# Hybrid layer with product-key experts on one core: a gathered row placed inside the weighing, the attention's normalisation placed earlier, one LayerNorm block split by tiles, and expert weights loaded 11 transfers ahead

## The chip, the cores and the metric

The kernel runs on one core of a Trainium2 chip. The metric is the device time of one execution in microseconds (us); lower is better. Engines are named as in the profile: PE (matrix multiply), PEld (its weight loads), DVE (vector), ACT (scalar), POOL (GpSimd), SP (its queue issues most transfers).

## The reference, cut to what matters

One layer: an input projection feeds a gated recurrence, a convolution and a grouped attention with rotary positions; their merged outputs go through a projection and a LayerNorm (norm 1); then come product-key experts and norm 2. The change touches the attention, norm 1 and above all the experts:

```python
v1, i1 = lax.top_k(s1, PEER_TOPK); v2, i2 = lax.top_k(s2, PEER_TOPK)
...
score, ci = lax.top_k(cand, PEER_TOPK)        # 16 of 16384 experts for each token and head
g = jax.nn.softmax(score, axis=-1)
act = jax.nn.gelu(jnp.einsum('thkd,td->thk', u_tab[expert], t))
return jnp.einsum('thk,thkd->td', g * act, v_tab[expert])
```

There are 512 tokens, 8 heads of 16 experts, and 16384 experts with two rows of 1024 numbers each (tables u and v).

## The kernel before, in words

All matrix products are made of three matmuls on numbers split into a high part (`whi`, `ph`, made by ACT) and a low part (`wlo`, `pl`, made by DVE as number minus high part). The order of work on PE, DVE, ACT and POOL is the order of the code; each of these engines works its list off strictly in order. The order of SP's transfers is made by a scheduler, but SP too works its list off in order.

**Experts.** The experts are done in two ways at once.

- Tokens 0 to 127 gather. For each of the 128 pairs of head and rank one transfer, issued by POOL, fetches 128 rows (512 KB, tile `raw`) of u, later of v. `gather_step` uses one such transfer: for u a product with the tokens (L1489), for v a multiply and add into `ttok` (L1497). I call one of these a row operation. 14 of the 256 are done before the stages below; the rest are spread over the steps below by a budget (`shares`), 1.18 in a step at first and 3.22 later.
- Tokens 128 to 511 are done densely: 128 groups of 128 experts. For group n, `first` multiplies the weights u(n) with the tokens (24 matmuls into `pa`), ACT applies the gelu (tile `a`), `weigh` multiplies it by the gates (`gr`, L1602) and splits the product into `ph` and `pl` (L137, L138), and `second` multiplies it with v(n) (18 matmuls into `acc`). For groups 0 to 70 the gelu output was made earlier and kept: 32 in SBUF (tile `arun`, named `gt` in the profile), 39 in DRAM (`ad`).

The main loop runs over steps i. Step i weighs group i + 1 and runs `second` for group i. I name three stretches of it. **Stage A1** is steps 0 to 31, whose activations lie in SBUF. **Stage A2** is steps 32 to 68, whose activations are read back from DRAM (192 KB each). **Stage B** is steps 69 to 122, each of which also runs one `first`.

Weights come through `wload`: one 512 KB transfer into one of three buffers `wraw` (L124), two halves cast by ACT (L129) and two low parts (L131). `fetch` calls it when a step wants the group. When `arun` has been read, its space takes the 11 tiles of norm 2 (`fin`), eight of which `prepare` fills by transfers of 512 KB, starting at i = 96 in the code; SP's list has them much earlier, where the space comes free. `prepare` then runs eight vector operations on them (L1679, L1682).

**Attention.** A slot n of 32 handles one head and block of queries: the softmax of slot n + 1 is started, the scores of n + 2 multiplied, and `turn` transposes the probabilities `P` of slot n. `norm` divides `P` by its sum (L947, L948). Parts of the next heads' projections, rotations (`rope`) among them, are slipped in as `early` and `late`.

**Norm 1.** `modulate` scales the transposed block by channel: eight 128x128 pieces in two tiles `tf` of four, some on DVE (L1172), some on ACT (L1170). PE's next products (`pu`) need the high part of block 3 (L1179).

Of the kernel before, what the change touches and what calls it, by code (L numbers as in the profile page):

```python
# [9 lines left out]
F32 = mybir.dt.float32  # L10
# [7 lines left out]
AF = mybir.ActivationFunctionType  # L18
# [4 lines left out]
T, TC, D, KT = 512, 256, 1024, 8  # L23
NB, NBC = T // 128, TC // 128
H = 8
# [69 lines left out]
def body(tc, I, O):  # L95
    nc = tc.nc
# [39 lines left out]
    def split(hi, lo, src):  # L136
        A.activation(hi, src, AF.Copy)  # L137
        V.tensor_sub(lo, src, hi.bitcast(F32))  # L138
# [76 lines left out]
    u = hc.tile([128, KT, T], F32, name="u")  # L215
# [105 lines left out]
    def go(*gens):  # L321
        for g in gens:
            next(g, None)
# [239 lines left out]
    def norm():  # L563

        bc = pms.tile([128, T], F32, name="ms")
        P.matmul(bc, ones[:, 0:1].to_broadcast([128, 128]), usum, start=True, stop=True)
        qsum = hp.tile([128, T], F32, name="scT")
        last = None
        for j in range(KT):
            uj = u[:, j, :]  # L570
            V.scalar_tensor_tensor(uj, bc, -1.0 / D, uj, op0=ALU.mult, op1=ALU.add)
            sq = hp.tile([128, T], F32, name="KM")
            A.activation(sq, uj, AF.Square)
            if j:
                G.tensor_add(qsum, last, sq)
            last = qsum if j else sq
            if j % 3 == 2:
                yield
        yield
        st = pms.tile([128, NB], F32, name="ms")  # L580
        for b in range(NB):
            P.matmul(st[:, b:b + 1], qsum[:, b * 128:(b + 1) * 128], ones, start=True, stop=True)
        t1 = const.tile([128, NB], F32, name="lt")
        rs = const.tile([128, NB], F32, name="lrs")
        pspow(rs, st, 1.0 / D, t1)
        yield
        uhl.extend([mp.tile([128, KT, T], F32R, name="uhi"), hc.tile([128, KT, T], F32R, name="og")])
        bc = pst.tile([128, NB, 128], F32, name="bc")
        for b in range(NB):
            P.matmul(bc[:, b, :], rs[:, b:b + 1].to_broadcast([128, 128]), ident, start=True, stop=True)  # L590
        bc = bc[:].rearrange("p b t -> p (b t)")
        V.tensor_mul(u[:, 0, :], u[:, 0, :], bc)
        yield
        for j in range(KT):
            uj = u[:, j, :]
            if j + 1 < KT:
                V.tensor_mul(u[:, j + 1, :], u[:, j + 1, :], bc)
            s = mp.tile([128, T], F32, name="ms", bufs=2)
            A.activation(s, uj, AF.Sigmoid, scale=chan['clg'][:, j:j + 1], bias=chan['clb'][:, j:j + 1])
            V.tensor_scalar(uj, uj, chan['clg'][:, j:j + 1], chan['clb'][:, j:j + 1], op0=ALU.mult, op1=ALU.add)  # L600
            V.tensor_mul(uj, uj, s)
            A.activation(uhl[0][:, j, :], uj, AF.Copy)
            if j:
                V.tensor_sub(uhl[1][:, j - 1, :], u[:, j - 1, :], uhl[0][:, j - 1, :].bitcast(F32))
            yield
        V.tensor_sub(uhl[1][:, KT - 1, :], u[:, KT - 1, :], uhl[0][:, KT - 1, :].bitcast(F32))
        yield
# [358 lines left out]
    def slot(n, early=(), late=(), mid=(), pre=()):  # L966

        h, b = divmod(n, NB)
        norm(h, b)
        if n + 1 < NB * H:  # L970
            softmax(*divmod(n + 1, NB))
        go(*pre)
        if n + 2 < NB * H:
            scores(*divmod(n + 2, NB))
        fetch_next()
        if b == 0 and h:
            out(h - 1)
        go(*early)
        fetch_next()
        go(*mid)  # L980
        turn(b)
        go(*late)
        fetch_next()

# [178 lines left out]
    def modulate(b, pts):  # L1163
        tfs = []
        for q_, pt in enumerate(pts):
            tf = op.tile([128, 4, 128], F32, name="tf", bufs=4)
            for i in range(4):
                j = q_ * 4 + i
                if j > 4 if b == 3 else q_:
                    A.activation(tf[:, i, :], pt[:, i, :], AF.Identity, scale=gs[:, j:j + 1], bias=bs[:, j:j + 1])  # L1170
                else:
                    V.tensor_scalar(tf[:, i, :], pt[:, i, :], gs[:, j:j + 1], bs[:, j:j + 1], op0=ALU.mult, op1=ALU.add)  # L1172
            tfs.append(tf)
        return tfs
# [94 lines left out]

    vrows = I['v'].rearrange("(a b) d -> a b d", b=128)  # L1270

    def fetch(item):
        kind, i = item
        src = {'q': I['wq'], 'u': I['uT'], 'v': None}[kind]
        src = vrows[i] if kind == 'v' else src[i]
        if kind != 'q':
            src = src.rearrange("p (k e) -> p k e", e=128)
        UV[item] = wload(src, SUBS[kind])

    ad = tc.dram_tile([NU - NA, 128, TD], F32, name="ad")  # L1280

# [309 lines left out]

    ph = {}

    def halves(i2, a_):
        names = ("raw", "raw") if i2 >= NT - 2 else ("ph", "pl")
        ph[i2] = [pp.tile([128, TD], F32R, name=n, bufs=RB[1] if n == "raw" else 2) for n in names]
        split(ph[i2][0], ph[i2][1], a_)

    def weigh(n, a_):

        v_ = a_.rearrange("p (b t) -> p b t", t=GB)
        V.tensor_tensor(v_, v_, gates[n // GN][:, :, n % GN, :], op=ALU.mult)  # L1602
        halves(n, a_)
        if n % GN == GN - 1:
            del gates[n // GN]
        read_gates(n)
# [21 lines left out]
    def shares(i):  # L1628

        n = min(2 * NS_, EARLY + int(share * sum(budget[:i + 1])))  # L1630
        out = [gather_step] * (n - gathered[1])
        gathered[1] = n
        return out

    todo = []

# [85 lines left out]
    for i in range(NT - LAST):  # L1722
        n = i + 1
        todo += shares(i)
        left = 6
        if NU <= n:
            fetch(('u', n + 1))
            left = 10
            a_ = first(n, left)
        else:  # L1730
            if n + 1 == NU:
                fetch(('u', NU))
            if NA <= n + 1 < NU:
                back[n + 1] = gap.tile([128, TD], F32, name="a", bufs=4)
                nc.sync.dma_start(back[n + 1], ad[n + 1 - NA])
            weigh(n, arun[:, n, :] if n < NA else back.pop(n)[:])
        if ('v', n) not in UV:
            fetch(('v', n))
        for m in range(2):
            for b in range(NB - 1):  # L1740
                second(i, b, m)
                some(6 - 3 * m - b)
        if NU <= n:
            weigh(n, a_[:])
        if i >= NT - 32:
            prepare(i - NT + 32)
        if gathered[0] == 2 * NS_ and 0 not in nst:
            residual(0, 0)
            residual(0, 1)
            moments(0)  # L1750
            norm2(0, 0)
            norm2(0, 1)
        del UV['v', i], ph[i]
# [42 lines left out]
```

## Time and profile before

| | before |
|---|---|
| median of 3 runs | 2436.23 us (2435.23 to 2440.38) |
| the profiled execution | 2440.56 us, span 2438.8 us |
| mean granted TensorE clock | 0.990 |
| busy over the span | PE 96%, PEld 83%, DVE 79%, ACT 43%, POOL 27% |
| bytes moved by the DMA engines | 452.66 MB |

A busy share is an average over stages with different limits, and PE's is also flattered, since the ends of pipelined matmuls are modelled and overlap. What a stage is worth is read from its own length, and from how far apart the same instruction starts in neighbouring steps.

### The profile page before, as it was taken

The numbers are of one execution on the slowest core, as the hardware profiler recorded it, in microseconds if no ns is written. First come the engines' busy times: TensorE is split into PE (matmuls) and PEld (weight loads), VectorE is DVE, ScalarE is ACT, GpSimd is POOL, SyncE is SP. The second block draws the span as 40 slices with busy tenths as digits, with TensorE's granted clock in tenths as the row PEclk, the third lists the DMA queues.
The fourth block names the chain that finished last, engine by engine and source line by source line (L and its number), as shares of the span: only waits on it lengthen the run. The fifth ranks groups of instructions, "written<-read, shape, count | busy, mean of one in ns | idle before, by whom it ended". The sixth has DMA issues, their size and how long they took to land.

```text
span 2438.8 us, 34766 instructions
## 1 busy us (share of the span) xinstructions
PE 2344.7 (96%) x12547; PEld 2022.8 (83%) x12547; DVE 1935.6 (79%) x3736; ACT 1043.3 (43%) x2294; POOL 648.6 (27%) x555
## 2 busy tenths in 40 slices
PE   7999999999999999999999999999989999999997
PEld 3888888887887777877999999987767888898886
DVE  7788888887875566564999699968878788889886
ACT  5544444443423444643366645533333333332333
POOL 6000000002111000041688301122323344444432
PEclk9999999999999999999999999999999999999999
DMA  6211111111482111242323379999999989998962
GB/s 241 74 61 61 60 54 61 61 61 64 163 303 76 35 35 35 70 145 81 104 98 111 123 259 324 327 331 307 349 354 348 351 320 336 339 333 317 337 220 93
DMA packets 156973, 452.66 MB, mean 186 GB/s; under 512 B 16256, under 2 KB 60672, under 8 KB 154624
## 3 DMA queue, kind: packets, MB, share of 16 engines
q1 hardware_dynamic: 106976, 278.33, 32.9%
q0 software_dynamic: 36864, 134.23, 15.5%
q10 hardware_dynamic: 12960, 37.87, 4.1%
q8 instruction: 99, 1.62, 0.3%
q14 instruction: 74, 0.61, 0.1%
HBM read 411.77 MB, written 37.03 MB: 184 GB/s over the span
## 4 chain that ended last, share of the span: by engine, by line
PE 60%; DVE 24%; DMA 7%; ACT 5%; issue 3%; POOL 2%; ACTq 0%; DVEq 0%; POOLq 0%; SPq 0%
PE mm L142 13%; PE mm L144 13%; PE mm L143 13%; DVE wlo L131 6%; DVE raw L1489 4%; DMA wraw<-in_v_dram 3%; PE sc L455 2%; PE pg L1539 2%; ACT whi L129 2%; PE acc L142 2%; PE acc L143 2%; PE acc L144 2%; ACT ph L137 2%; DMA wraw<-in_uT_dram 2%; DVE ttok L1497 2%
## 5 line engine op out<-in xcount | busy, mean ns | idle before, releaser
L131 DVE TENSOR_TENSOR wlo<-wraw,whi 128x512 fp32r<-128x512 f32 x687 | 465.1, 719 | 156.3 <-ACT whi L129 155.0
L142 PE MATMUL mm<-xh,wlo 128*128 128x512 f32 (+1 forms) x1448 | 555.9, 384 | 12.4 <-POOL wlo L131 3.8
L143 PE MATMUL mm<-xl,whi 128*128 128x512 f32 (+1 forms) x1448 | 536.9, 371 | 2.1 <-DVE xl L1180 0.9
L144 PE MATMUL mm<-xh,whi 128*128 128x512 f32 (+1 forms) x1448 | 537.3, 371 | 0.0
L129 ACT ACTIVATE whi<-wraw 128x512 fp32r<-128x512 f32 x784 | 448.5, 621 | 98.7 <-DMA wraw<-in_v_dram 22.6
L142 PE MATMUL acc<-whi,pl 128*128 128x512 f32 x756 | 300.6, 398 | 24.1 <-DVE pl L138 17.2
L142 PEld LDWEIGHTS mm<-xh,wlo 128*128 128x128 f32 x1448 | 273.9, 189 | 46.0 <-POOL wlo L131 4.5
L144 PEld LDWEIGHTS mm<-xh,whi 128*128 128x128 f32 x1448 | 273.0, 189 | 37.1
L143 PEld LDWEIGHTS mm<-xl,whi 128*128 128x128 f32 x1448 | 273.9, 189 | 35.4 <-DVE xl L316 2.1
L143 PE MATMUL acc<-wlo,ph 128*128 128x512 f32 x756 | 301.5, 399 | 1.8 <-DVE wlo L131 0.7
L144 PE MATMUL acc<-whi,ph 128*128 128x512 f32 x756 | 297.5, 394 | 0.0
L1478 POOL DMA_INDIRECT raw<-in_u_dram,idx x128 | 146.9, 1148 | 470.2 <-DVE act L1489 411.1
L1478 POOL DMA_INDIRECT raw<-in_v_dram,idx x128 | 160.5, 1254 | 191.3 <-DVE ttok L1497 154.4
L142 PEld LDWEIGHTS acc<-whi,pl 128*128 128x128 f32 x756 | 143.2, 189 | 63.4 <-ACT whi L129 18.3
L137 ACT ACTIVATE ph<-a 128x384 fp32r<-128x384 f32 x94 | 49.4, 525 | 335.7 <-DVE a L1602 312.7
L550 DVE SCALAR_TENSOR_TENSOR u<-up,dw,u 128x512 f32<-128x512 f32 x240 | 179.5, 748 | 4.9
L143 PEld LDWEIGHTS acc<-wlo,ph 128*128 128x128 f32 x756 | 143.5, 190 | 42.9 <-DVE wlo L131 14.1
L144 PEld LDWEIGHTS acc<-whi,ph 128*128 128x128 f32 x756 | 143.5, 190 | 28.5
L1497 DVE SCALAR_TENSOR_TENSOR ttok<-raw,act,ttok 128x1024 f32<-128x1024 f32 x127 | 162.9, 1283 | 3.1
L142 PE MATMUL pa<-xh,wlo 128*128 128x384 f32 x456 | 155.3, 340 | 5.2 <-DVE wlo L131 5.2
L131 POOL TENSOR_TENSOR wlo<-wraw,whi 128x512 fp32r<-128x512 f32 x97 | 132.8, 1391 | 89.3 <-ACT whi L129 87.3
L144 PE MATMUL pa<-xh,whi 128*128 128x384 f32 x456 | 154.6, 339 | 0.0
(423 smaller groups left out, 4236.1 us busy)
## 6 DMA issues: line engine op xcount, KB each, us to landing
wraw<-in_uT_dram SPq DMA_DIRECT2D x128, 512.0 KB, 5.1
wraw<-in_v_dram SPq DMA_DIRECT2D x128, 512.0 KB, 5.8
wraw<-in_w_in_dram SPq DMA_DIRECT2D x96, 512.0 KB, 3.3
gd<-gs ACTq DMA_DIRECT2D x16, 1536.0 KB, 7.7
gr<-gd SPq DMA_DIRECT2D x60, 288.0 KB, 9.2
ohi<-in_w_adaT_dram SPq DMA_DIRECT2D x32, 512.0 KB, 5.4
wraw<-in_wq_dram SPq DMA_DIRECT2D x16, 512.0 KB, 3.3
ad<-a ACTq DMA_DIRECT2D x39, 192.0 KB, 4.7
```

The costliest lines, as they stand in the source:

```text
L129: A.activation(hi, r, AF.Copy)
L131: subs[i].tensor_sub(lo, r, hi.bitcast(F32))
L137: A.activation(hi, src, AF.Copy)
L142: P.matmul(out, ll, rh, start=first, stop=False)
L143: P.matmul(out, lh, rl, start=False, stop=False)
L144: P.matmul(out, lh, rh, start=False, stop=last)
L455: P.matmul(x_.ps[:, b, :], x_.KM[:, b * 128:(b + 1) * 128], ap3(x_.QP, T + b * 128, [2 * w_, 64 // w_], [w_ - T, 2], [1, w_]), start=True, ...
L550: V.scalar_tensor_tensor(acc, up[:, i:i + T], dw[:, j, i:i + 1], acc, op0=ALU.mult, op1=ALU.add)
L1478: G.indirect_dma_start(out=r, out_offset=None, in_=I['u'] if n < NS_ else I['v'], in_offset=bass.IndirectOffsetOnAxis(ap=idx0[:, n % NS_:n ...
L1489: V.tensor_tensor_reduce(out=r, in0=r, in1=ttok, scale=1.0, scalar=0.0, op0=ALU.mult, op1=ALU.add, accum_out=act[:, s_:s_ + 1])
L1497: V.scalar_tensor_tensor(ysb, r, act[:, s_:s_ + 1], ysb, op0=ALU.mult, op1=ALU.add)
L1539: P.matmul(ps[:, i, :], o3[:, q_, :, i], o1[:, i, :], start=q_ == 0, stop=q_ == 1)
```

## The change: what it does

Four edits. In the attention, `norm` for slot n + 1 stands right behind `turn` of slot n, ahead of the `late` parts. In norm 1, block 3 is cut as the others: four pieces on DVE, four on ACT, so that each tile `tf` is written by one engine. In `weigh`, one row operation stands between the gate product and the low part (`between`; in stage B it is the last of the step's row operations, held back). And weights of stage B are loaded up to 11 transfers ahead into the space of `arun`; `prepare` starts at i = 110.

```diff
@@ slot
-        norm(h, b)
+        if n == 0:
+            norm(h, b)
...
         turn(b)
+        if n + 1 < NB * H:
+            norm(*divmod(n + 1, NB))
         go(*late)
@@ modulate
-                if j > 4 if b == 3 else q_:
+                if q_:
@@ halves, weigh
+        hi, lo = ph[i2]
+        A.activation(hi, a_, AF.Copy)
+        between()
+        V.tensor_sub(lo, a_, hi.bitcast(F32))
@@
+    DEEP = 11
+    BACK = NT - 20
+    early = {}
+    line = [w for n in range(NU + 1, BACK) for w in (('u', n + 1), ('v', n))]
+    wide = []
+
+    def load(w):
+
+        if w not in early:
+            if line and w == line[0]:
+                line.pop(0)
+            fetch(w)
+        else:
+            UV[w] = wload(None, SUBS[w[0]], early.pop(w))
+        if w[1] < NU:
+            return
+        if not wide:
+            t_ = gap.tile([128, NA, TD], F32, name="gt")[:].rearrange("p i t -> p (i t)")
+            wide.extend([t_[:, j * D:(j + 1) * D].rearrange("p (k e) -> p k e", e=128) for j in range(DEEP)])
+        for _ in range(2 if w[0] == 'u' else 1):
+            if line and len(early) < DEEP:
+                w_ = line.pop(0)
+                early[w_] = wide[0]
+                wide.append(wide.pop(0))
+                nc.sync.dma_start(early[w_], place(w_))
@@ main loop
-            fetch(('u', n + 1))
+            load(('u', n + 1))
             left = 10
+            held = todo.pop() if todo else lambda: None
             a_ = first(n, left)
...
-            weigh(n, arun[:, n, :] if n < NA else back.pop(n)[:])
+            weigh(n, arun[:, n, :] if n < NA else back.pop(n)[:], todo.pop(0) if todo else lambda: None)
         if ('v', n) not in UV:
-            fetch(('v', n))
+            load(('v', n))
...
-            weigh(n, a_[:])
-        if i >= NT - 32:
-            prepare(i - NT + 32)
+            weigh(n, a_[:], held)
+        if i >= NT - 18:
+            prepare(i - NT + 18)
```

The built programs show where this lands. On DVE, a step of stage A2 with one row operation was this (the row operation is the pair of L1489, which writes `raw` and reads its sum into `act`):

```order
L1602 TENSOR_TENSOR a<-a,gr 128x384
L138 TENSOR_TENSOR pl<-a,ph 128x384
L131 TENSOR_TENSOR wlo<-wraw,whi 128x512 x2
L1489 ISA raw,act<-raw,ttok 128x1024
L1489 ISA act 128x1
L1602 TENSOR_TENSOR a<-a,gr 128x384
```

and is now this:

```order
L1608 TENSOR_TENSOR a<-a,gr 128x384
L1492 ISA raw,act<-raw,ttok 128x1024
L1492 ISA act 128x1
L1603 TENSOR_TENSOR pl<-a,ph 128x384
L131 TENSOR_TENSOR wlo<-wraw,whi 128x512 x2
L1608 TENSOR_TENSOR a<-a,gr 128x384
```

The row operation has moved in between the product and `pl`; the count is the same.

On SP, in stage A2 where the space of `arun` comes free, the list of before has the tiles of norm 2 (`gt` from `ln` and `x1d`, eight transfers, here the first four) between the reads of `a` and the loads of v:

```order
L1735 DMA a<-ad 128x384
L124 DMA wraw<-in_v_dram 128x1024
L1668 DMA gt<-in_ln_g_dram 128x1024
L1735 DMA a<-ad 128x384
L124 DMA wraw<-in_v_dram 128x1024
L1668 DMA gt<-in_ln_b_dram 128x1024
L1735 DMA a<-ad 128x384
L124 DMA wraw<-in_v_dram 128x1024
L1668 DMA gt<-in_ln_g_dram 128x1024
L1668 DMA gt<-in_ln_b_dram 128x1024
L1735 DMA a<-ad 128x384
```

The changed list has weights of stage B at the same place, eleven transfers in all:

```order
L1768 DMA a<-ad 128x384
L124 DMA wraw<-in_v_dram 128x1024
L1665 DMA gt<-in_uT_dram 128x1024
L1768 DMA a<-ad 128x384
L124 DMA wraw<-in_v_dram 128x1024
L1665 DMA gt<-in_v_dram 128x1024
L1768 DMA a<-ad 128x384
L1665 DMA gt<-in_uT_dram 128x1024
L124 DMA wraw<-in_v_dram 128x1024
L1665 DMA gt<-in_v_dram 128x1024
L1768 DMA a<-ad 128x384
```

The tiles of norm 2 now stand in stage B, near step 107, behind the last of the early loads. Before, the list had only weights and gates there:

```order
L124 DMA wraw<-in_uT_dram 128x1024
L1590 DMA gr<-gd 128x3x192 x3
L124 DMA wraw<-in_v_dram 128x1024
L1590 DMA gr<-gd 128x3x192
L1590 DMA gr<-gd 128x4x192
L124 DMA wraw<-in_uT_dram 128x1024
L124 DMA wraw<-in_v_dram 128x1024
```

and now:

```order
L1665 DMA gt<-in_v_dram 128x1024
L1593 DMA gr<-gd 128x3x192 x4
L1593 DMA gr<-gd 128x4x192
L1700 DMA gt<-in_ln_g_dram 128x1024
L1700 DMA gt<-in_ln_b_dram 128x1024
L1700 DMA gt<-in_ln_g_dram 128x1024
L124 DMA wraw<-in_v_dram 128x1024
L1700 DMA gt<-in_ln_b_dram 128x1024
L1709 DMA gt<-x1d 128x1024
L124 DMA wraw<-in_uT_dram 128x1024
L1709 DMA gt<-x1d 128x1024
L124 DMA wraw<-in_v_dram 128x1024
```

The first of them waits there until the last early load has been cast.

## Rows read from the trace of the kernel before

**Rows 1.** Windows: stages A1, A2, B; engines' busy us (instructions), clock, DMA share, GB/s.

```profile
1603.15:1742.55 139.40, 134.98 (x576) 106.33 (x577) 113.76 (x199) 50.61 (x96) 40.76 (x38) 1.00 0.93 321
1742.55:1912.05 169.50, 159.81 (x667) 123.28 (x667) 135.08 (x237) 58.60 (x112) 48.71 (x44) 0.99 0.99 361
1912.05:2391.45 479.40, 463.06 (x2285) 416.76 (x2284) 408.17 (x542) 169.93 (x330) 202.97 (x161) 0.98 0.87 313
```

**Rows 2.** Windows of stages A1 and B, instructions that touch `acc` alone (PE, PEld, DVE).

```profile
1603.15:1742.55 139.40, 134.98 (x576) 106.33 (x577) 0.00 (x0) 1.00 0.93 321
...
1912.05:2391.45 479.40, 237.59 (x973) 184.05 (x972) 0.00 (x0) 0.98 0.87 313
```

**Rows 3.** Timeline, PE, stages A1 and A2: start, duration, [idle before <-releaser].

```profile
1736.25 0.40 PE L144 MATMUL acc<-whi,ph 128*128 128x512 f32 x1
...
1740.34 0.39 PE L144 MATMUL acc<-whi,ph 128*128 128x512 f32 x1
...
1755.62 0.47 PE L142 MATMUL acc<-whi,pl 128*128 128x512 f32 x1 [0.48 <-DVE pl L138]
```

**Rows 4.** Timeline, DVE, a step of stage A2 with two row operations.

```profile
1751.39 1.22 DVE L1489 CUSTOM_DVE_ANT_0 raw<-raw,ttok 128x1024 f32<-128x1024 f32 x1
...
1753.68 0.55 DVE L1602 TENSOR_TENSOR a<-a,gr 128x384 f32<-128x384 f32 x1
1754.91 0.56 DVE L138 TENSOR_TENSOR pl<-a,ph 128x384 fp32r<-128x384 f32 x1 [0.67 <-ACT ph L137]
...
1756.64 1.22 DVE L1489 CUSTOM_DVE_ANT_0 raw<-raw,ttok 128x1024 f32<-128x1024 f32 x1
```

**Rows 5.** Groups by line, DVE, stage B: busy us, mean ns | idle before, releaser.

```profile
L1497 DVE SCALAR_TENSOR_TENSOR ttok<-raw,act,ttok 128x1024 f32<-128x1024 f32 x127 | 162.9, 1283 | 3.1
L131 DVE TENSOR_TENSOR wlo<-wraw,whi 128x512 fp32r<-128x512 f32 x220 | 145.0, 701 | 29.2 <-ACT whi L129 29.2
...
L138 DVE TENSOR_TENSOR pl<-a,ph 128x384 fp32r<-128x384 f32 x54 | 30.2, 560 | 35.5 <-ACT ph L137 35.5
...
L1679 DVE TENSOR_TENSOR gt<-gt 128x1024 f32<-128x1024 f32 x4 | 4.9, 1216 | 0.0
```

**Rows 6.** Timeline, ACT, two neighbouring steps of stage B without a stall.

```profile
2115.61 0.50 ACT L1651 ACTIVATE a<-pa 128x384 f32<-128x384 f32 x1 [2.11 <-PE pa L144]
...
2123.92 0.49 ACT L1651 ACTIVATE a<-pa 128x384 f32<-128x384 f32 x1 [2.40 <-PE pa L144]
```

**Rows 7.** Timeline, ACT, the longest stall of stage B.

```profile
1951.44 1.15 ACT L129 ACTIVATE whi<-wraw 128x512 fp32r<-128x512 f32 x2 [8.61 <-DMA wraw<-in_uT_dram]
```

**Rows 8.** Waits of PE in stage B: us in total, times, longest.

```profile
PE acc L142 <- DVE pl L138: 11.1, 9, 3.3
PE pa L142 <- DVE wlo L131: 5.2, 2, 3.2
```

**Rows 9.** Windows with a DMA backlog, and one at the lower clock; columns as in rows 1.

```profile
1750.00:1800.00 50.00, 43.73 (x175) 32.85 (x174) 35.86 (x62) 15.33 (x29) 12.32 (x11) 0.97 1.03 394
...
1930.00:1950.00 20.00, 19.62 (x98) 17.26 (x96) 11.84 (x22) 4.20 (x8) 9.10 (x7) 1.00 1.03 388
...
2368.00:2371.40 3.40, 3.37 (x11) 3.37 (x12) 3.40 (x3) 1.19 (x3) 3.32 (x3) 0.53 0.21 77
```

**Rows 10.** DMA: the queue of the gathered rows (packets, MB, share), and one issue (KB, us to landing).

```profile
q0 software_dynamic: 36864, 134.23, 15.5%
...
wraw<-in_v_dram SPq DMA_DIRECT2D x128, 512.0 KB, 5.8
```

**Rows 11.** Waits of PE in the attention, 760 to 1110 us.

```profile
PE pt L956 <- DVE P L948: 6.1, 9, 1.2
```

**Rows 12.** Timeline, DVE, ACT and PE, block 3 of norm 1.

```profile
1133.41 1.68 DVE L1172 TENSOR_SCALAR tf<-pt,gs,bs 128x128 f32<-128x128 f32 x5
...
1135.13 1.16 ACT L1170 ACTIVATE tf<-pt,bs,gs 128x128 f32<-128x128 f32 x3 [2.56 <-DVE tf L1172]
...
1136.85 0.69 PE L142 MATMUL pu<-xh,wlo 128*128 128x384 f32 x1 [3.21 <-ACT xh L1179]
```

More of the change, by code (lines that the diff above doesn't have):

```diff
@@ L1270, in body, with place @@
     vrows = I['v'].rearrange("(a b) d -> a b d", b=128)
+    def place(item):
+        kind, i = item
+        src = {'q': I['wq'], 'u': I['uT'], 'v': vrows}[kind][i]
+        return src if kind == 'q' else src.rearrange("p (k e) -> p k e", e=128)
     def fetch(item):
[L1273 to L1278, printed above, removed]
+        UV[item] = wload(place(item), SUBS[item[0]])
     ad = tc.dram_tile([NU - NA, 128, TD], F32, name="ad")
@@ L1592, in body, with halves, weigh @@
     ph = {}
-    def halves(i2, a_):
+    def halves(i2, a_, between):
         names = ("raw", "raw") if i2 >= NT - 2 else ("ph", "pl")
         ph[i2] = [pp.tile([128, TD], F32R, name=n, bufs=RB[1] if n == "raw" else 2) for n in names]
-        split(ph[i2][0], ph[i2][1], a_)
-    def weigh(n, a_):
+        hi, lo = ph[i2]
+        A.activation(hi, a_, AF.Copy)
+        between()
+        V.tensor_sub(lo, a_, hi.bitcast(F32))
+    def weigh(n, a_, between=lambda: None):
         v_ = a_.rearrange("p (b t) -> p b t", t=GB)
         V.tensor_tensor(v_, v_, gates[n // GN][:, :, n % GN, :], op=ALU.mult)
-        halves(n, a_)
+        halves(n, a_, between)
         if n % GN == GN - 1:
```

## The prediction

> **What bounds the kernel now.** I read first the windows of the three stages that the change touches, then the distance between neighbouring steps, then who waits for whom. In stages A1, A2 and B (788 of 2439 us) PE is busy for 94 to 97% of the time, DVE for 80 to 85% [rows 1]. That looks like PE's bound, but the steps say otherwise. A step of `second` is 18 matmuls, and in a stretch without a stall the same matmul comes again after 1740.34 - 1736.25 = 4.09 us [rows 3]; I use 4.1. The counts of matmuls (576 and 973, by 18) give 32 steps for A1 and 54 for B [rows 2]; the 37 between them are A2's. So the stages take 4.36, 4.58 and 8.88 us a step. In stage B the undisturbed step is 2123.92 - 2115.61 = 8.31 us [rows 6]. Against these paces A1 loses 139.4 - 131.2 = 8.2 us, A2 169.5 - 151.7 = 17.8 us, and B 479.4 - 448.7 = 30.7 us, 56.7 us together. That is all that can be won there.
>
> Who loses it? DVE. In a step with two row operations, DVE starts its first row operation at 1751.39 and the next step's at 1756.64: 5.25 us for a step for which PE needs 4.1 [rows 4], and PE waits for `pl` just then [rows 3]. Within the step DVE stands idle for 0.67 us between the gate product and the low part, since ACT must make `ph` in between [rows 4]. With 38 + 44 row operations issued in 69 steps [rows 1] and some 1.2 us each [rows 4], DVE needs per step 113.76/32 + 0.67 = 4.22 us in A1 and 135.08/37 + 0.67 = 4.32 us in A2 [rows 1]: more than PE's 4.1. In B, DVE is busy for 408.2 us, waits 35.5 us for `ph` and 29.2 us for cast weights, together 473 of 479 us [rows 1, 5]. PE's waits there are for `pl` (9 times, 11.1 us) and for `wlo` (twice, 5.2 us) [rows 8]. The longest stall begins with u weights that landed late: ACT idles 8.6 us for them [rows 7]. The rest of B's loss is the clock: a mean of 0.98 over 479.4 us [rows 1] is about 9.6 us. It is lost in short stretches at the lower of the clock's two levels (1.2 for 2.4 GHz), as behind the stall at the end of B, where 0.53 is granted over 3.4 us [rows 9]; each such stretch costs some 1.7 us.
>
> **Part by part: the row operation inside `weigh`.** No instruction is added. The idle 0.67 us is filled by an operation of 1.2 to 1.3 us [rows 4, 5], so DVE needs 113.76/32 = 3.56 us in A1 and 135.08/37 = 3.65 us in A2, below 4.1. `pl` comes some 0.6 us later behind its product than before; what hides that is the pair of `ph` and `pl` buffers, since DVE may weigh a group a whole step ahead, and DVE now has 0.45 us or more to spare per step. A1 then goes at PE's pace but for its start, where the first v weights are awaited; I leave 2 us: 139.4 - 131.2 - 2 = **6.2 us won**. (Bounds: 0 if another wait takes over, 8.2.)
>
> **Stage A2 and the early loads.** Here the transfers matter. A step moves 0.524 MB of v [rows 10] and 0.197 MB each of gates and of activations (128x384 numbers); 44 row transfers of 134.23/256 = 0.524 MB each [rows 1, 10] come on top. That is 57.0 MB in A2, and with the eight tiles of norm 2 (4.2 MB) 61.2 MB, or 361 GB/s over 169.5 us, which is what the window shows [rows 1]: the account is complete. The change puts eleven loads (5.8 MB) where the eight were: 62.8 MB. The best rate over 50 us is 394 GB/s [rows 9], so A2 needs at least 159.3 us; PE needs 151.7. Transfers, not DVE, will set A2. I take 162 us, somewhat over the lower bound, since the eleven loads stand at the start of the stage, ahead of v loads in SP's list: 169.5 - 162 = **7.5 us won**. (Bounds: 159.3 at 394 GB/s; 173.9 at the 361 GB/s of before, a loss of 4.4.)
>
> The Trainium skill, page "DMA: Bandwidth & Descriptors", section Specifications, gives about 358 GB/s as what one core gets from HBM, and that speaks against this part. By it A2 would take 62.8/0.358 = 175 us (an estimate from that page) and the whole 2415 us. The trace does not agree: it has 394 GB/s over 50 us and 388 over 20 us [rows 9].
>
> **Stage B.** With up to eleven loads in stock, a late u (the 8.6 us of rows 7) no longer stops ACT and DVE; loads land in 5.8 us at the median [rows 10], and the stock covers five steps of two loads each. The 35.5 us wait for `ph` is covered by the held row operation for as long as there are rows. Together this leaves DVE with about 408 us of work in 449 us of PE's, and the clock's loss goes with the stalls. What stays: the block at the end, where the first result tile is finished on DVE while a load stands behind the output's transfer in SP's list (the second of the `wlo` waits, 2 us of rows 8, a last wait for `pl`, and 1.7 us for a stretch at the lower clock); 4.7 us. What is added: the eight tiles of norm 2 now load near step 107, 4.2 MB or 10.6 us of the DMA engines at 394 GB/s, and `prepare`'s eight vector operations (8 x 1.22 = 9.7 us [rows 5]) move from steps 100 to 107 to steps 114 to 121. The loads are covered as far as transfers leave room (B's mean is 313 GB/s [rows 1], more while rows are fetched); three of the eight operations come when no row is left. Covered wholly, the two cost nothing; uncovered 10.6 + 9.7 = 20.3 us. I take 4.2, since DVE gains 0.65 us a step and PE's deadline for `pl` is several us off. B: 448.7 + 4.7 + 4.2 = 457.6, **21.8 us won**.
>
> **Attention.** PE waits for the normalised `P` 9 times, 6.1 us in all, at most 1.2 [rows 11]. In each of the three groups of slots there is one place where the normalisation already followed the low part of the slot before directly on DVE; nothing changes there, and I take these for the longest waits: 6.1 - 3 x 1.2 = 2.5 us are left to win. The moved operation now delays what it has overtaken (rotations, parts of the values), each of which PE also awaits in places. Between -2.5 and +2.5; I take **1.0 won**, since a rotation waits for PE's own product first, and DVE is free until then.
>
> **Norm 1.** DVE writes five pieces from 1133.41 in 1.68 us, and ACT, whose three share a tile with the fifth, starts at 1135.13; PE stood idle from 1136.85 - 3.21 = 1133.64, when its transposes had ended [rows 12]. With a tile to itself ACT starts at about 1133.65 and needs four pieces, 4/3 x 1.16 = 1.55 us: done at 1135.2 instead of 1136.29. **1.1 us won**; at worst 0.4 lost (a piece more, no earlier start).
>
> **The sum.** 6.2 + 7.5 + 21.8 + 1.0 + 1.1 = 37.6 us off the profiled execution's 2440.6 gives 2403.0. That execution is 4.3 us above the median of 2436.2; part of this will be stalls that I count as won, so the median falls by less than 37.6. I take 34: **2402 us**.
>
> **Rivals.**
>
> - *Transfers take over.* A2 goes on at 361 GB/s and ends at 173.9 us. B is not hit by that: 313 GB/s x 479.4 us = 150 MB [rows 1], less three loads, needs 411 us at 361, under PE's 449. 162 to 173.9 is 12 us: 2414. For it speaks a DMA share of 0.99 in A2 [rows 1]; against it the 394. The figure of the Trainium skill, page "DMA: Bandwidth & Descriptors", section Specifications, would give nearly this (2415).
> - *The moved tiles of norm 2 come dear.* Their loads stand ahead of v and u loads when the stock is used up, and the vector operations fall among the last rows: 16 us instead of 4.2: 2414, or 2418 with two more stretches at the lower clock. For it: no idle room in SP's list there. Against it: while SP waits for the last early load, DMA is nearly free.
> - *Slower: rows come late.* `pl` now stands behind a row operation. If rows land late, because eleven loads compete with them, DVE waits and PE with it. The trace has no such wait (3.1 us idle before L1497 in all [rows 5]). DVE has about 0.6 us a step to spare; lateness beyond that costs directly, over some 119 steps. It eats the 34 us from 0.9 us a step on; at 1.0, 0.4 x 119 = 48 us, so 2402 + 48 = 2450.
> - *The change doesn't do it.* Something else than the 0.67 us holds the steps, and loads are not late for want of room: 2434.
>
> **Chances.** Forecast 0.60 (2390 to 2411), transfers 0.18, norm 2's tiles 0.12, rows late 0.05, no effect 0.03, others 0.02. A difference of 0.2% (about 5 us) is what a measurement of this kernel can tell from none. Faster 0.92, same 0.03, slower 0.05. The range goes from 2390 (A2 at its bound, starts and moved work at nothing: 2.7 + 2 + 4.2, and the 3.6 us that I took off) to 2420 (either of the two dearer cases, with the clock); that leaves out under 0.2.
>
> **What would show it.** `pl` without a wait for `ph`; steps of 4.1 in A1; A2 near 162 us with a rate above 361 GB/s; steps of 8.31 in B with no wait of ACT for weights before step 107; eight loads near step 107 and what PE waits for behind them. The prediction is wrong if DVE waits for rows, if A2 gets no shorter, or if B loses more than 10 us behind step 107.

## The result, and the profile after

| | after |
|---|---|
| median of 4 runs | 2403.45 us (2399.67 to 2403.72) |
| ratio to before, 95% interval | 0.9857 (0.984 to 0.9874) |
| the profiled execution | 2403.31 us, span 2401.5 us |
| mean granted TensorE clock | 0.993 |

With one more run of before beside it (2437.91 us), before has a median of 2437.07 us of 4 runs. The change makes the kernel faster by 33.6 us.

The windows of the three stages answer to [rows 1], with the same columns:

```profile
1600.30:1733.67 133.37, 132.15 (x576) 107.98 (x577) 115.45 (x204) 50.72 (x96) 37.47 (x38) 1.00 0.97 345
1733.67:1896.21 162.54, 155.98 (x667) 125.44 (x666) 132.35 (x238) 61.10 (x113) 43.82 (x44) 0.99 1.03 383
1896.21:2354.18 457.97, 451.30 (x2285) 409.92 (x2284) 396.62 (x536) 170.00 (x328) 201.29 (x160) 1.00 0.89 322
```

A1 is 6.0 us shorter, A2 7.0 and B 21.4, 34.4 together. The instructions of PE and DVE are the same to a handful. In the three stages DVE is idle for 21.8 us less (109.5 instead of 131.3), and busy for 12.6 us less (644.4 instead of 657.0). Of the 37.3 us that the span lost, 2.9 us lie ahead of A1.

The timeline of DVE in a step of stage A2 answers to [rows 4]; it has one row operation between the two gate products, where [rows 4] has two:

```profile
1741.46 0.55 DVE L1608 TENSOR_TENSOR a<-a,gr 128x384 f32<-128x384 f32 x1
1741.94 1.22 DVE L1492 CUSTOM_DVE_ANT_0 raw<-raw,ttok 128x1024 f32<-128x1024 f32 x1
1743.08 0.55 DVE L1603 TENSOR_TENSOR pl<-a,ph 128x384 fp32r<-128x384 f32 x1
1743.55 1.29 DVE L131 TENSOR_TENSOR wlo<-wraw,whi 128x512 fp32r<-128x512 f32 x2
1744.75 0.55 DVE L1608 TENSOR_TENSOR a<-a,gr 128x384 f32<-128x384 f32 x1
```

Behind the gate product comes a row operation, and `pl` follows it at once, with no bracket for an idle time. Not every step is like this: the two that follow it in the trace still show 0.30 and 0.65 us there, and the idle time before `pl` falls from 20.8 to 9.8 us in A1 and from 26.8 to 5.7 us in A2. From one gate product to the next DVE needs 1744.75 - 1741.46 = 3.29 us here, and it is busy for 132.35/37 = 3.58 us a step on average in A2, less than the 4.09 us that PE needs for a step [rows 3]. It has turned from the engine that sets the step into one that waits: PE, which waited for `pl` for 6.0 us in A1 and A2 together before, has no such wait listed there now.

The groups of DVE in stage B answer to [rows 5] (busy us, mean ns | idle before, releaser):

```profile
L1500 DVE SCALAR_TENSOR_TENSOR ttok<-raw,act,ttok 128x1024 f32<-128x1024 f32 x127 | 162.5, 1280 | 1.7
L131 DVE TENSOR_TENSOR wlo<-gt,whi 128x512 fp32r<-128x512 f32 x144 | 92.8, 686 | 34.2 <-ACT whi L129 33.9 <-issue 0.3
L131 DVE TENSOR_TENSOR wlo<-wraw,whi 128x512 fp32r<-128x512 f32 x72 | 49.6, 730 | 20.1 <-ACT whi L129 20.1
...
L1603 DVE TENSOR_TENSOR pl<-a,ph 128x384 fp32r<-128x384 f32 x54 | 29.7, 551 | 2.0 <-ACT ph L1601 2.0
```

The idle time before `pl` fell from 35.5 to 2.0 us. But the idle time before the weights' low parts (`wlo`) rose from 29.2 to 54.3 us, although two thirds of them (144 of 216) now read a tile `gt` that was loaded ahead. In a kernel that is faster this is no loss: it is where DVE now waits for the others. The row operations wait for their rows for 1.7 us in all. What PE still waits for in B, to be read beside [rows 8]:

```profile
PE acc L142 <- DVE pl L1603: 3.9, 3, 2.3
PE pa L142 <- DVE wlo L131: 2.8, 1, 2.8
```

What is left in B stands in two places. Here are some of ACT's gelus, of which each step of B has one, and one of its waits for weights:

```profile
1904.71 0.49 ACT L1683 ACTIVATE a<-pa 128x384 f32<-128x384 f32 x1 [3.10 <-PE pa L144]
...
2220.36 0.49 ACT L1683 ACTIVATE a<-pa 128x384 f32<-128x384 f32 x1 [3.74 <-PE pa L144]
...
2227.86 1.15 ACT L129 ACTIVATE whi<-wraw 128x512 fp32r<-128x512 f32 x2 [4.08 <-DMA wraw<-in_uT_dram]
...
2274.03 0.49 ACT L1683 ACTIVATE a<-pa 128x384 f32<-128x384 f32 x1 [0.90 <-PE pa L142]
...
2315.57 0.49 ACT L1683 ACTIVATE a<-pa 128x384 f32<-128x384 f32 x1 [1.18 <-PE pa L144]
2330.42 0.47 ACT L1683 ACTIVATE a<-pa 128x384 f32<-128x384 f32 x1
...
2337.84 0.47 ACT L1683 ACTIVATE a<-pa 128x384 f32<-128x384 f32 x1
```

From the gelu of step 69 (1904.71) to that of step 107 (2220.36) all 38 steps take 8.31 us [rows 6]. From 2220.36 to 2274.03 lie six steps, 53.67 us instead of 6 x 8.31 = 49.86: this is behind the place where the tiles of norm 2 now load, ahead of the weights. And 2315.57 to 2330.42 is 14.85 us for one step, of which the next makes up a little (7.42): the block at the end, in which the first result tile is finished on DVE. SP's list stands still before the first of these tiles until the last early load has been cast, and the v and u loads behind them in the list stand with it (SP's waits: us in total, times, longest):

```profile
SPq L1700 <- DVE wlo L131: 29.7, 1, 29.7
```

### The profile page after: what moved, and what is told of

Its sections match the earlier page's. It is cut to its first block, busy times and chain, and to the rows that moved or that the text cites. A ratio compares the mean times of both kernels' runs of the same rounds, so it can differ in the third digit from the quotient of the medians.

```text
span 2401.5 us, 34806 instructions
## 1 busy us (share of the span) xinstructions
PE 2326.3 (97%) x12547; PEld 2020.9 (84%) x12547; DVE 1923.5 (80%) x3735; ACT 1046.2 (44%) x2295; POOL 639.5 (27%) x555
## 4 chain that ended last, share of the span: by engine, by line
PE 73%; DVE 15%; DMA 7%; issue 2%; ACT 2%; POOL 2%; SPq 0%; ACTq 0%; DVEq 0%; POOLq 0%
PE mm L142 13%; PE mm L144 13%; PE mm L143 13%; PE acc L143 5%; PE acc L144 5%; PE acc L142 5%; DMA wraw<-in_v_dram 3%; PE pa L142 3%; PE pa L144 3%; PE pa L143 3%; DVE wlo L131 2%; PE sc L455 2%; PE pg L1542 2%; DVE eb L1346 1%; DMA wraw<-in_uT_dram 1%
## 5 line engine op out<-in xcount | busy, mean ns | idle before, releaser
L131 DVE TENSOR_TENSOR wlo<-wraw,whi 128x512 fp32r<-128x512 f32 x543 | 371.8, 727 | 168.3 <-ACT whi L129 161.8
L129 ACT ACTIVATE whi<-wraw 128x512 fp32r<-128x512 f32 x640 | 366.8, 622 | 110.0 <-DMA wraw<-in_v_dram 41.9
L1481 POOL DMA_INDIRECT raw<-in_u_dram,idx x128 | 135.0, 1055 | 459.6 <-DVE act L1492 406.8
L1500 DVE SCALAR_TENSOR_TENSOR ttok<-raw,act,ttok 128x1024 f32<-128x1024 f32 x127 | 162.5, 1280 | 1.7
L1492 DVE CUSTOM_DVE_ANT_0 raw<-raw,ttok 128x1024 f32<-128x1024 f32 x128 | 155.1, 1219 | 0.0
```

Of the source, the lines that this page charges most:

```text
L129: A.activation(hi, r, AF.Copy)
L131: subs[i].tensor_sub(lo, r, hi.bitcast(F32))
L1481: G.indirect_dma_start(out=r, out_offset=None, in_=I['u'] if n < NS_ else I['v'], in_offset=bass.IndirectOffsetOnAxis(ap=idx0[:, n % NS_:n ...
L1492: V.tensor_tensor_reduce(out=r, in0=r, in1=ttok, scale=1.0, scalar=0.0, op0=ALU.mult, op1=ALU.add, accum_out=act[:, s_:s_ + 1])
L1500: V.scalar_tensor_tensor(ysb, r, act[:, s_:s_ + 1], ysb, op0=ALU.mult, op1=ALU.add)
```

## The experiments

My theory was the prediction's: in A1 and A2 the idle 0.67 us on DVE sets the step; in B the wait for `ph` and late weights cost apart from each other, and the row operation cures the one, the early loads the other. The rivals were that one of the two edits does all of it, and that the place of the row operation matters for the rows rather than for the idle time. All kernels here compute the whole reference. The table has the medians (before ran beside them: 2436.14 us median of 13 with the first four, 2437.72 median of 7 with the last four), the ratio to before with its interval, and the lengths of the stages in the profiled execution. Its last two columns cut B in two, by the gelus of steps 69, 107 and 122; at PE's pace these stretches take 38 x 8.307 = 315.7 and 15 x 8.307 = 124.6 us.

| kernel | median us | ratio (95%) | A1 | A2 | B | steps 69 to 107 | 107 to 122 |
|---|---|---|---|---|---|---|---|
| before | 2437.07 | | 139.4 | 169.5 | 479.4 | 338.0 | 133.1 |
| after | 2403.45 | 0.9857 (0.984 to 0.9874) | 133.4 | 162.5 | 458.0 | 315.7 | 134.1 |
| 1 row operation alone | 2401.63 | 0.9855 (0.9838 to 0.9871) | 134.7 | 158.6 | 462.0 | 321.6 | 132.1 |
| 2 early loads alone | 2425.39 | 0.9953 (0.9936 to 0.9969) | 140.2 | 167.6 | 465.9 | 315.7 | 141.8 |
| 3 attention and norm 1 alone | 2433.18 | 0.9995 (0.9983 to 1.0008) | 140.0 | 167.8 | 476.7 | 337.4 | 131.0 |
| 4 after, 5 loads ahead | 2398.22 | 0.9841 (0.9814 to 0.9868) | 134.0 | 157.4 | 462.5 | 315.7 | 138.6 |
| 5 low parts of v in the gap | 2423.7 | 0.9935 (0.9917 to 0.9952) | 134.8 | 162.4 | 477.2 | 337.1 | 131.8 |
| 6 after, space in quarters | 2389.56 | 0.9803 (0.9786 to 0.9819) | 135.5 | 152.5 | 454.7 | 315.7 | 130.8 |
| 7 quarters, no early loads | 2392.45 | 0.9806 (0.9788 to 0.9824) | 136.0 | 155.7 | 457.2 | 319.4 | 129.5 |
| 8 as 6, end block spread | 2387.04 | 0.9793 (0.9776 to 0.9811) | 137.8 | 153.7 | 450.3 | 315.7 | 126.4 |

Each kernel has one profiled execution, and it need not be a typical one: that of kernel 1 took 2409.1 us, 7.5 above its median, that of kernel 5 2429.1, 5.4 above, that of kernel 3 2429.81, 3.4 below. Kernel 3 changes nothing in A2 and B, and yet they are 1.7 and 2.7 us shorter in its profile than in that of before. Differences of this size between the stages of two profiles prove little.

**1. The row operation alone.** On the kernel before, only this (with `between` in `halves` as in the change):

```diff
-            weigh(n, arun[:, n, :] if n < NA else back.pop(n)[:])
+            weigh(n, arun[:, n, :] if n < NA else back.pop(n)[:], todo.pop(0) if todo else lambda: None)
...
+            held = todo.pop() if todo else lambda: None
...
-            weigh(n, a_[:])
+            weigh(n, a_[:], held)
```

> The kernel before with one edit alone: the row operation between gate product and low part. If the vector engine's 0.67 us wait a step was what held stages A1 and A2, A1 is 133 us as with the whole change, and A2 is set by transfers: 61.2 MB at 394 GB/s is 155 us, so about 158. In stage B the wait for ph is covered, but weights still come late (29 us of the vector engine's idle time before): 463 to 466 us. Whole: about 2403 to 2407. The rival, that in stage B the early loads did the work, has B at 472 us or more and the whole at 2413 or more. The other rival, that the wait held nothing, has A1 at 139 us.

Measured: 2401.63 us, the whole gain of the change. The windows of A2 and B:

```profile
1739.38:1898.00 158.62, 154.50 (x667) 125.79 (x666) 131.62 (x235) 60.09 (x113) 43.70 (x44) 0.99 1.03 382
1898.00:2360.00 462.00, 452.07 (x2285) 409.61 (x2284) 397.92 (x538) 170.90 (x329) 204.95 (x160) 1.00 0.89 323
```

A2 is shorter than after's by 3.9 us, about what its 1.6 MB less (three loads) make at 382 GB/s, and B is longer by 4.0. (A1 came out 1.7 us above what was expected, B 1.0 and the whole 1.4 below.) The loads are as late as before. Here are ACT's gelus of steps 69 and 107 of this kernel, with two of the late u loads between them, to be read beside [rows 7]:

```profile
1906.49 0.49 ACT L1654 ACTIVATE a<-pa 128x384 f32<-128x384 f32 x1 [2.67 <-PE pa L144]
...
1933.95 1.15 ACT L129 ACTIVATE whi<-wraw 128x512 fp32r<-128x512 f32 x2 [7.42 <-DMA wraw<-in_uT_dram]
...
2135.97 1.15 ACT L129 ACTIVATE whi<-wraw 128x512 fp32r<-128x512 f32 x2 [7.70 <-DMA wraw<-in_uT_dram]
...
2228.11 0.49 ACT L1654 ACTIVATE a<-pa 128x384 f32<-128x384 f32 x1 [0.48 <-PE pa L144]
```

In the kernel before, the same two gelus are these:

```profile
1920.62 0.49 ACT L1651 ACTIVATE a<-pa 128x384 f32<-128x384 f32 x1 [1.88 <-PE pa L144]
...
2258.62 0.47 ACT L1651 ACTIVATE a<-pa 128x384 f32<-128x384 f32 x1
```

ACT's waits for u weights in B, first of this kernel, then of the one before, are longer in all, and there are as many:

```profile
ACT whi L129 <- DMA wraw<-in_uT_dram: 32.1, 7, 8.9
...
ACT whi L129 <- DMA wraw<-in_uT_dram: 21.0, 7, 8.6
```

But the 38 steps take 321.6 us instead of 338.0, so they lose 6.0 us to their pace instead of 22.3. The three steps around the wait of 7.42 us lose 2.1 us, where the three around the 8.61 of [rows 7] lost 6.3. The other two long waits (7.70 and, behind step 107, 8.91) cost 3.7 and 4.2 us. So a late load that finds DVE with time to spare is caught up in part: 10.0 us of late loads are left in B, while DVE's wait for `ph` is down to 1.9 us.

**2. The early loads alone** (`load`, `place`, `DEEP`, and `prepare` at i = 110, on the kernel before; the lines here are a part).

```diff
+        if not wide:
+            t_ = gap.tile([128, NA, TD], F32, name="gt")[:].rearrange("p i t -> p (i t)")
...
-        if i >= NT - 32:
-            prepare(i - NT + 32)
+        if i >= NT - 18:
+            prepare(i - NT + 18)
```

> The kernel before with the early loads alone (and prepare at i = 110). If the vector engine holds A1, it stays at 139 us. A2 has both the vector engine (4.32 x 37 = 160 us) and 62.8 MB: 172 to 176 us, slower than before (169.5). Stage B loses the late weights but keeps the wait for ph: the vector engine needs 408 + 35.5 = 444 of 449 us, so nearly no room; 462 to 468 us. Whole: 2424 to 2434. The rival, that late weights alone made stage B's loss, has B at 458 us and the whole at about 2420.

Measured: 2425.39 us; A1 is unchanged and B is shorter by 13.5 us. A2 is not longer, against the expectation; its 1.9 us less are no more than two profiles differ. The gelus of steps 69 and 107, and DVE's idle time before `pl` in B:

```profile
1921.12 0.49 ACT L1677 ACTIVATE a<-pa 128x384 f32<-128x384 f32 x1 [2.08 <-PE pa L144]
...
2236.77 0.49 ACT L1677 ACTIVATE a<-pa 128x384 f32<-128x384 f32 x1 [2.67 <-PE pa L144]
...
L138 DVE TENSOR_TENSOR pl<-a,ph 128x384 fp32r<-128x384 f32 x54 | 30.2, 560 | 35.5 <-ACT ph L137 27.1 <-issue 8.5
```

The idle time before `pl` is the 35.5 us of before, and still the 38 steps from 69 to 107 take 315.65 us, PE's pace: the early loads alone remove all that was lost there. So that wait costs nothing in B by itself; what cost was a late load on a DVE that had no time to catch it up. The length of B fell into the expected range for another reason than I gave: its 17.2 us over the pace all lie behind step 107, where the tiles of norm 2 and the block at the end stand. With the row operation the early loads win 6.0 us up to step 107, lose 1.9 behind it and 3.9 in A2. The two edits overlap: 10.8 us and 34.5 us apart, 33.6 us together.

**3. The two early edits alone** (`norm` behind `turn`; `if q_:` in `modulate`).

> The kernel before with the two early edits alone (normalisation behind the transposes, norm 1 on two tiles). From the attention's start to stage A1 shorter by 2 to 4 us, no other stage changed; whole about 2433, not to be told from before by the times. The rival, that these edits carry a good part of the gain, has 2425 or less.

Measured: 2433.18 us of 10 runs, not to be told from before. In the trace the attention and norm 1 (from the first matmul behind 757.3 us to norm 1's `pu`) take 376.1 us instead of 379.5. From there to A1 it is 462.4 instead of 466.3, so that the whole stretch is 7.3 us shorter, more than the 2 to 4 expected; the last section says what these 3.9 us go with.

**4. Five loads ahead instead of eleven.**

```diff
-    DEEP = 11
+    DEEP = 5
```

> The changed kernel with 5 early loads in stock instead of 11. If transfers set stage A2 (62.8 MB now, 162.5 us), six loads less are 3.1 MB or 8 us at 394 GB/s: 155 to 157 us. If 5 in stock are enough for stage B, it stays at 458 us and the whole is 2396 to 2399. The rivals: the depth is needed (B grows by more than 4 us), or A2's loss is not the transfers' (A2 stays above 160 us).

Measured: A2 is 157.4 us, 5.1 shorter, for six transfers (3.1 MB) fewer in it. At the 383 GB/s that A2 sustains, 3.1 MB are 8.2 us; PE's pace, 151.7, is near. B is 462.5, 4.5 longer, but not since the stock runs out: up to step 107 its steps take 315.65 us, as with eleven. The loss lies behind that, where SP's list reaches the tiles of norm 2 some 7 us earlier (2199.40 instead of 2206.11) and ACT waits 7.4 us for a u load at 2263 us, behind the last of the early ones; what makes that load late is not shown. The whole is 2398.22 us, and its interval overlaps after's. Bytes decide A2; for the steps up to 107 five loads in stock are enough.

**5. The low parts of v in the gap, the row operation where it was.** On the kernel before, the loading of v is cut in two, and its two subtractions stand between gate product and `pl`:

```diff
+            low = begin_load(('v', n)) if ('v', n) not in UV else lambda: None
-            weigh(n, arun[:, n, :] if n < NA else back.pop(n)[:])
+            weigh(n, arun[:, n, :] if n < NA else back.pop(n)[:], low)
```

> The kernel before, but in stages A1 and A2 the two low parts of the step's v weights stand between gate product and low part, their casts on ACT ahead of it; no row operation is moved, stage B and the loads are as before. If it is the vector engine's idle 0.67 us a step that held A1 and A2, any work that fills it does: A1 133 to 135 us, A2 156 to 161, B 477 to 480 as before, the whole 2418 to 2424. The rival, that the row operation's earlier place (and so an earlier fetch of the next row) made the gain, has A1 at 139 and the whole at 2434 to 2437.

Measured: A1 takes 134.8 us, as with the row operation (134.7), and the whole 2423.7, as expected. A2, 162.4, is a little longer than expected, and B, where this kernel changes nothing, is as before to 2.2 us. It is the filling of the idle time that counts, whatever fills it, not the earlier use of the rows. (This kernel also casts the v weights earlier on ACT, ahead of `ph`; no run moves those casts alone.)

**6. The space of the kept activations in four tiles.** In the changed kernel `arun` is one tile of 32 activations, so the first early load waits until the last has been read, at the end of A1. Here it is four tiles of eight:

```diff
-    arun = gap.tile([128, NA, TD], F32, name="gt")
+    arun = [gap.tile([128, 8, TD], F32, name=f"gt{p_}") for p_ in range(4)]
...
-            t_ = gap.tile([128, NA, TD], F32, name="gt")[:].rearrange("p i t -> p (i t)")
-            wide.extend([t_[:, j * D:(j + 1) * D].rearrange("p (k e) -> p k e", e=128) for j in range(DEEP)])
+            parts_ = [gap.tile([128, 8, TD], F32, name=f"gt{p_}")[:].rearrange("p i t -> p (i t)") for p_ in range(4)]
+            wide.extend([parts_[j // 3][:, j % 3 * D:(j % 3 + 1) * D].rearrange("p (k e) -> p k e", e=128) for j in range(DEEP)])
```

Groups of three loads now begin in A1, behind its steps 8, 16 and 24; the bytes of the two stages together are the same. The tiles of norm 2, which follow in the same space, are cut in the same way and so come free in quarters too.

> The changed kernel with the kept activations in four tiles of eight instead of one of 32: their space comes free in quarters from step 8 on, so nine of the eleven early loads go out in stage A1, where the transfers leave room (1.34 MB a step of 4.1 us is 327 GB/s). Same bytes, same instructions on the engines. If A2's 11 us over the matmul's pace are transfers without room, A2 falls to 152 to 156 us, A1 stays at 133 to 135, B at 458: the whole 2394 to 2398. The rival, that A2's stalls come from something else (order on SP, late reads of the activations), has A2 above 160 and the whole at 2402.

Measured: 2389.56 us.

```profile
1597.69:1733.23 135.54, 133.24 (x576) 107.75 (x577) 114.90 (x204) 51.39 (x96) 38.85 (x39) 1.00 1.01 374
1733.23:1885.75 152.52, 152.07 (x667) 124.76 (x666) 132.77 (x238) 60.23 (x113) 43.76 (x44) 1.00 1.02 378
```

A2 falls to 152.5 us, PE's pace, and A1 takes the transfers for 2.2 us more: it had room, at 345 GB/s in the changed kernel. B is 3.3 us shorter, all of it behind step 107, where SP's list now stands for at most 12.9 us at a time before a tile of norm 2, not 29.7. The whole is faster than expected (2394 to 2398); 2.6 of the 13.7 us between the two profiles lie ahead of A1.

**7. Quarters, the row operation and the two early edits, but no early loads.** The tiles of norm 2 load in A1 again.

> Row operation inside, the two early edits, no early loads; the space of the kept activations in quarters, so that the tiles of norm 2 load in stage A1. A2 152 to 156 us; B as with the row operation alone, 462 us; the whole 2395 to 2399. If the early loads are worth 4 us in B, this kernel lies 4 us above the one with quarters and early loads.

Measured: 2392.45 us, with B at 457.2, both shorter than expected. Kernel 6 is 2.9 us faster, less than these runs can tell apart, so what the early loads add once the space comes free in time is not shown. In the two profiles they take off 3.7 us up to step 107, and cost 1.3 behind it.

**8. As 6, with the block at the end spread over four steps.**

```diff
+    ending = [partial(residual, 0, 0), partial(residual, 0, 1), partial(moments, 0), lambda: (norm2(0, 0), norm2(0, 1))]
...
-        if gathered[0] == 2 * NS_ and 0 not in nst:
-            residual(0, 0)
-            residual(0, 1)
-            moments(0)
-            norm2(0, 0)
-            norm2(0, 1)
+        if gathered[0] == 2 * NS_ and ending:
+            ending.pop(0)()
```

> The kernel with quarters and early loads, and the block that finishes the first result tile spread over four steps (two residual halves, the moments, the two halves of norm 2) instead of standing in one. If the 5.5 us that step 120 takes over its pace are this block, on the vector engine and in SP's list, B falls from 458 to 453 to 455 us and the whole by as much: 2390 to 2394. The rival, that the wait only moves to the steps behind, leaves B at 457 or more.

Measured: 2387.04 us, the shortest median of all. The steps at the end of B now keep their pace, 8.31 us each:

```profile
2313.50 0.49 ACT L1683 ACTIVATE a<-pa 128x384 f32<-128x384 f32 x1 [3.84 <-PE pa L144]
2321.80 0.49 ACT L1683 ACTIVATE a<-pa 128x384 f32<-128x384 f32 x1 [3.84 <-PE pa L144]
2330.11 0.49 ACT L1683 ACTIVATE a<-pa 128x384 f32<-128x384 f32 x1 [3.84 <-PE pa L144]
```

B is 450.3 us, within 2 us of PE's 448.7. The stretch behind step 107 takes 126.4 instead of 130.8 us, so that the block cost what it did is shown in the trace; whether the gain over kernel 6 in whole runs is real is not, since the intervals overlap.

## Why the prediction was right, and where it was not

The total was right: 37.6 us forecast off the profiled execution, 37.3 measured, and 2402 for a median of 2403.45. The three large terms were right one by one; that the small ones ahead of A1 come to 2.9 us where 2.1 were forecast is partly luck, as told below.

- **A1** (forecast 133.2, measured 133.4): right, with its reason. Kernel 2 leaves the idle time and gains nothing there; kernels 1 and 5 fill it in two ways and gain the same. The average of 4.22 us a step that I gave for DVE would explain only 3.8 of the 8.2 us lost (and 8.1 of A2's 17.8); a step with two row operations took 5.25 us [rows 4], and an average hides such steps.
- **A2** (162, measured 162.5): right. Transfers set it, as kernels 4 and 6 show from both sides. The rate over the whole stage was 383 GB/s, so the rival in which it stays at 361 fell: that was the rate at which a slower DVE asked, not the most that could be had (kernel 1 moves the bytes of before at 382). The Trainium skill, page "DMA: Bandwidth & Descriptors", section Specifications, gives a limit of about 358 GB/s for one core, as half of a stack's 716 GB/s. The trace does not agree for this core: 383 GB/s over 162.5 us.
- **B** (457.6, measured 458.0): right, and the mechanism with it: no late u stops a step up to 107, and `pl` no longer waits for `ph`. What I read wrongly is who lost the time before. I added DVE's busy time, its wait for `ph` and its wait for weights to 473 of 479 us, as if each had to be cured. Kernel 2 keeps the wait for `ph` and loses nothing up to step 107; kernel 1 keeps the late loads and loses 6.0 of the 22.3 us there. Either edit does most of the work: the row operation alone brought 17.4 of the 21.4 us, the early loads alone 13.5, and the loads on top of the row operation 4.0, as much as they cost in A2. The clock recovered with the row operation alone, too: 1.00 in kernel 1.
- **The tiles of norm 2 and the end block** (4.2 and 4.7 us left to them): near. The six steps from 2220.36 lost 3.8 us; the end block lost 5.7 (22.27 us for the two steps from 2315.57, less 16.61).
- **Attention** (1.0 won): the mechanism as described, the size unclear. Waits of PE from 758 to 1108 us:

```profile
PE pt L956 <- DVE P L948: 3.5, 3, 1.2
PE mm L897 <- DVE vl L138: 2.8, 3, 0.9
```

The wait for `P` fell by 2.6 us [rows 11], about the 2.5 that I held to be winnable; but with the same attention, other profiles show from none (kernel 6) to 3.5 us of it (after, 8), so the three waits that I took to be fixed are not. In its place the overtaken low part `vl` is waited for, 2.8 us instead of the 0.6 of before. The stretch from the attention's start to `pu` shrank by 4.9 us, but near 788 us the profiles differ in the clock. Among those with 0.89 over 16 us there, the stretch takes 379.5 us without the two early edits (before, 1, 2) and 376.1 to 376.3 with them (3, 4, 6, 7). Among those with 1.00 it takes 378.0 without (5) and 374.6 to 374.7 with them (after, 8). So the two edits win 3.3 us at either clock: 1.1 for norm 1, and 2.2 for the attention, twice the forecast. In the profile of after, another 1.6 us were won there by the clock and 1.6 lost ahead of the attention, which starts at 758.89 instead of 757.31 us.
- **Norm 1** (1.1 won): right for the wait itself, which fell from 3.21 us [rows 12] to 2.12; the last section shows that more may go with it:

```profile
1133.53 0.44 PE L142 MATMUL pu<-xh,wlo 128*128 128x384 f32 x1 [2.12 <-ACT xh L1182]
```

- **Slower, because rows come late**: fell. 1.7 us of idle time before the row operations of B.

The early loads, then, show no gain in the kernel as it was changed: its median and that of kernel 1, which lacks them and the two early edits, lie 1.8 us apart, less than executions of one kernel differ (by 4 us for after, 8.7 for kernel 1). No run has the two early edits and the row operation, but no early loads, with the space in one tile. In B they do what they were made for; the bytes in A2 and the tiles of norm 2 behind step 107 take it back. What helped was to start the transfers in A1, where there is room, whether these are early loads (kernel 6) or the tiles of norm 2 (kernel 7); the single tile keeps the space locked until its last reader.

## What to carry to other kernels

Where an engine works its list in order and hands a value to another engine and back, put an independent operation into the gap. If that engine sets the pace, this counts until the next engine sets it: here filling 0.67 us of idle time brought 0.19 us a step in A1, since PE's pace came next. Idle times listed under several releasers don't add up as gains: here either of two cures brought most of what both brought. Cure one, measure, and only then price the next. Where a stage has a known pace, compare the lengths of its single steps: that showed here which steps lost the time, which no sum of idle times did. Space that is to be reused for loads should be cut into tiles that come free as they are read, so that the loads fall where the transfers have room.

## What the runs showed of the hardware

The transfers of one core went on at 374 to 383 GB/s for 135 to 163 us on end (374 in A1 and 378 in A2 of kernel 6, 376 in A2 of kernel 4, 383 in A2 of after), where A2 went at 361 before.

The stretch from norm 1's `pu` to stage A1, where no kernel here changes more than the tiles that the activations are written to, takes 466.1 to 466.8 us in the four profiles without the norm 1 edit (before, 1, 2, 5). With the edit it takes 462.4 to 462.5 us in four (3, 4, 6, 7), 464.0 in kernel 8, and 466.8 in the changed kernel. These times go with the clock. Here are 7 us around `pu`, first of before, where PE had been idle for 3.21 us, then of kernel 3, where it had been idle for 2.11:

```profile
1136.00:1143.00 7.00, 6.02 (x18) 5.65 (x19) 3.17 (x8) 2.84 (x5) 0.55 (x1) 0.51 0.18 75
1133.02:1140.02 7.00, 5.78 (x32) 5.55 (x33) 3.17 (x8) 2.83 (x5) 0.55 (x1) 1.00 0.18 75
```

The granted clock is 0.51 in the one and 1.00 in the other, and PE runs 18 matmuls in the one and 32 in the other. It is at 0.51 to 0.76 there in all four profiles with the longer wait, and at 1.00 in four of the six with the shorter one; after and kernel 8 have 0.76. So norm 1's edit may be worth up to 4 us more than its 1.1, in executions in which the clock then stays up; with one profile for each kernel that is a likely reading and not shown.

A second such place is near 1345 us. The changed kernel and kernel 6 differ there:

```profile
1340.00:1350.00 10.00, 7.35 (x27) 7.03 (x26) 9.90 (x46) 1.52 (x3) 9.19 (x13) 0.66 0.29 106
```

is the changed kernel, with a granted clock of 0.66, and this kernel 6, with 1.00:

```profile
1340.00:1350.00 10.00, 7.35 (x42) 7.03 (x41) 9.90 (x47) 3.40 (x15) 9.00 (x13) 1.00 0.31 100
```

PE runs 27 matmuls in the one and 42 in the other. Both stand behind the same idle time of 2.65 us (first the changed kernel, then kernel 6), so the wait alone does not decide it:

```profile
1343.63 0.69 PE L142 MATMUL mm<-xh,wlo 128*128 128x384 f32 x1 [2.65 <-POOL wlo L131]
1343.81 0.44 PE L142 MATMUL mm<-xh,wlo 128*128 128x384 f32 x1 [2.65 <-POOL wlo L131]
```

These differences, some 4 us, go with short stretches at the lower of the clock's two levels (1.2 for 2.4 GHz) behind such waits. They are as large as the small terms of the forecast, so a few us in one profile can't be booked on an edit before the clock has been compared. Whether executions of one kernel, which differ by some 4 us, do so for the same cause is not shown: only one of each was traced.
